# Own buffers and early loads for the opening weights, squares of x on ScalarE, in a hybrid decoder layer

## The chip, the cores and the metric

The kernel runs on one core of a Trainium2 chip. A core has TensorE (PE: matmuls; PEld: its weight loads), VectorE (DVE), ScalarE (ACT), GpSimd (POOL) and SyncE (SP, which here only issues DMAs), each with its own queue that it works through in order. Semaphores tie the queues together. 16 DMA engines move data from the main memory (HBM) into the on-chip memory (SBUF); matmuls write into PSUM banks.

The metric is the device time of one execution in microseconds, the median of several runs. Lower is better.

## What is computed

One decoder layer in float32 on 256 tokens of width 2048. The opening that is changed here is the first step of the mixer: a norm of x and the projection of the normed x.

```python
def rms_norm(x, g):
    xf = x.astype(jnp.float32)
    y = xf * lax.rsqrt(jnp.mean(xf * xf, axis=-1, keepdims=True) + RMS_EPS)
    return (y * g).astype(x.dtype)
...
    proj = h @ w_in
    mlstm_p, rwkv_p, gate_p = split_cols(proj, (MLSTM_TOTAL, RWKV_TOTAL, GATE_TOTAL))
...
for l in range(DEPTH):
    h = rms_norm(x, mix_pre_norm[l])
    y = hybrid_mixer(h, ...)
    x = x + rms_norm(y, mix_post_norm[l])
    h = rms_norm(x, xattn_pre_norm[l])
    m = rms_norm(mem, mem_norm[l])
    x = x + rms_norm(cross_attention(h, m, ...), xattn_post_norm[l])
    h = rms_norm(x, ffn_pre_norm[l])
    x = x + rms_norm(conv_glu_ffn(h, ...), ffn_post_norm[l])
```

`w_in` has 10536 columns. 384 of them, the narrow ones (the ranks of the RWKV decay, its rate and its gate, and the mLSTM gates, padded), are gathered into an own tensor `w_sm`. They are the opening block.

## The kernel before

**Products.** Features lie on the 128 partitions, so x is 16 feature tiles of 128 x 256 tokens. Every float32 product is made of three matmuls with a high and a low half of each operand: high x high, high weights x low x, low weights x high x. The halves of x are `hh` and `hl`, made by `split_gain` (L235): ScalarE writes the high half, `x * gain` rounded, and VectorE subtracts it from `x * gain`. The halves of a weight chunk are `wh` and `wl`, made by `Feed.hi` (L343, a ScalarE cast) and `Feed.lo` (L352, a VectorE subtraction). The norm's division comes after the projection: the squares of x are summed beside the products (`st0`, a `Stat`), and the evacuation multiplies the PSUM banks by the reciprocal root.

**Blocks and chunks.** The program is a list of blocks, one after the other. Each has a list of weight chunks (`srcs`), the x halves, and an evacuation. The opening block (L1278) has 8 chunks of 2 feature tiles x 384 columns (384 KB); the next ones, of `w_in`, 8 chunks of 2 x 512 columns (512 KB). `run` (L369) goes through the chunks and writes out the order of every queue: at chunk i it calls the block's `pre` hook, makes the halves up to chunk i + 1 and then i + 3, asks for the DMA of chunk i + 6, and then issues the matmuls of chunk i.

**Loads.** `Feed.dma` (L324) puts every chunk into one of three shared buffers (tag `raw`). SP issues the loads in program order, and a load waits until the subtraction (L357) of the chunk three before it has read the buffer. x comes in 8 loads of 2 feature tiles (`x_load`, L471). `run` starts with four loads of x and three of weights alternately; the others are issued in the first call of the hook and later.

**The hook.** `pre_sm` (L474) first issues 12 calls of a dummy matmul (`keep_warm`), then for the first three chunks the split of x, the split of the weights, and the next loads, and from then on one split of x per chunk (three chunks ahead). `x_piece` (L459) has, beside the splits, the squares: GpSimd multiplies two feature tiles by themselves (L464, L467) and adds them to the sum (L468).

**Side work.** Evacuations and the chains behind them are generators. `Spread.half` (L103) is called twice per chunk and takes one piece of the first of them, as long as a running account of ScalarE's and VectorE's time allows. `sm_evac` (L508) is the opening block's: it folds the sum (`Stat.finish`), waits three pieces, sums over partitions with TensorE (`st`), waits three more, spreads the root over the partitions (`stb`, `rb`), and then works on the two banks. The tag `big` has two buffers, which the kernel first uses for `KR` and `BK` in the evacuation of a later block (L691).

**The parameters** (`par`, 189 columns; the first 16 are the gain `mixg`) come with one load on ScalarE's queue (L193), the constants `con` and the two halves of `up` with loads that the hooks place between the chunks' (L486, L490, L492).

Of the kernel before, what the change touches and what calls it, by code (L numbers as in the profile page):

```python
# [9 lines left out]
F32 = mybir.dt.float32  # L10
# [5 lines left out]
P = 128  # L16
# [20 lines left out]
NPAR = _o  # L37
# [108 lines left out]
def _layer(ctx, tc, nc, d, dbg):  # L146
    act, dve = Meter(nc.scalar, 200.0, 0.83), Meter(nc.vector, 70.0, 1.04)
# [14 lines left out]
    def big(name, shape=None, dt=F32):  # L162
        return mp.tile(shape or [P, KD, S], dt, tag="big", bufs=2, name=name)
# [19 lines left out]
    def keep_warm(n):  # L183

        q = aux("warm", [P, P])
        for _ in range(n):
            mm(q, ones.broadcast_to((P, P)), ones.broadcast_to((P, P)))
# [2 lines left out]
    x0 = [U("x0"), U("x1")]  # L190
    xq = [x0[c // 4][:, c % 4 * 2:c % 4 * 2 + 2] for c in range(8)]
    par = cp.tile([P, NPAR], F32, name="par")
    act.dma_start(par, d["par"])  # L193
    con = cp.tile([P, NCON], F32, name="con")
    up = C("up", "bg0", [P, 1024])

    def pcol(n, i=0, w=1):
        return par[:, PC[n] + i:PC[n] + i + w]
# [36 lines left out]
    def split_gain(hi, lo, src, g):  # L235
        act.activation(hi, src, AF.Identity, scale=g)
        dve.scalar_tensor_tensor(lo, src, g, hi, op0=ALU.mult, op1=ALU.subtract)
# [80 lines left out]
    class Feed:  # L318
        def __init__(self):
            self.src = [s for b in blocks for s in b["srcs"]]  # L320
            self.kind = [b["kind"] for b in blocks for s in b["srcs"]]
            self.raw, self.st, self.nd, self.ns, self.nl = {}, {}, 0, 0, 0

        def dma(self, upto):  # L324
            while self.nd <= min(upto, len(self.src) - 1):
                s = self.src[self.nd]
                r = wp.tile(list(s.shape), F32, tag="raw", bufs=3, name="raw")
                sp.dma_start(r, s)
                self.raw[self.nd] = r
                self.nd += 1  # L330
# [12 lines left out]
        def hi(self, upto):  # L343
            while self.ns <= min(upto, len(self.src) - 1):
# [4 lines left out]
                self.st[self.ns] = [wh, None]  # L349
                self.ns += 1  # L350

        def lo(self, upto):  # L352
            self.hi(upto)
            while self.nl <= min(upto, len(self.src) - 1):
                r = self.raw.pop(self.nl)
                wl = self.staged("wl", r, self.nl)
                nc.vector.tensor_sub(wl, r, self.st[self.nl][0])  # L357
                self.st[self.nl][1] = wl
                self.nl += 1
# [8 lines left out]

    def run():  # L369
        feed = Feed()  # L370
        for c in range(4):
            x_load(c)
            feed.dma(min(c, 2))
        i = 0
        pend = []
        for b in blocks:
            if len(pend) >= 2:
                side.need(pend[-2])
            if b["before"]:
                b["before"]()  # L380
            nm = b["cols"] // P
            if b["kind"] == "fm":
                banks = [b["pool"]("fm", [P, 2, S]) for _ in range((nm + 1) // 2)]
            else:
                banks = [b["pool"]("tm") for _ in range(2 * (b["cols"] // 512))]
            nk = sum(s.shape[1] for s in b["srcs"])
            k = 0
            nt = len(b["srcs"]) if b["bankwise"] else b["tail"]
            if nt:
                b["srcs"], tail = b["srcs"][:-nt], b["srcs"][-nt:]  # L390
            for ci, s in enumerate(b["srcs"]):
                if b["pre"]:
                    b["pre"](ci, feed)
                feed.lo(i + 1)
                side.half()
                side.more = lambda: feed.hi(i + 2)
                ahead = b["xs"](k)
                feed.lo(i + 3)
                feed.dma(i + 6)
                wh, wl = feed.st.pop(i)  # L400
                for kj in range(s.shape[1]):
                    xh, xl = b["xs"](k) if kj else ahead
                    first, last = k == 0, k == nk - 1
                    if b["kind"] == "fm":
                        for m in range(nm):
                            o = banks[m // 2][:, m % 2]
                            a, c = wh[:, kj, m * P:(m + 1) * P], wl[:, kj, m * P:(m + 1) * P]
                            mm(o, a, xh, start=(first and m % 2 == 0), stop=False)
                            mm(o, a, xl, start=False, stop=False)
                            mm(o, c, xh, start=False, stop=last)  # L410
                            if nm == 8 and m == 3:
                                side.half()
                    else:
                        for g, o in enumerate(banks):
                            tm_products(o, g * P * 512 // b["cols"], g * 512 % b["cols"], (wh[:, kj], wl[:, kj], xh, xl),
                                        first, last)
                            if len(banks) == 4 and g == 1:
                                side.half()
                    k += 1
                    if kj + 1 < s.shape[1]:  # L420
                        side.half()
                i += 1
            if nt:

                feed.lo(i + nt - 1)
                steps = []
                for s in tail:
                    w = feed.st.pop(i)
                    for kj in range(s.shape[1]):
                        steps.append((w[0][:, kj], w[1][:, kj]) + tuple(b["xs"](k)))  # L430
                        k += 1
                    i += 1
                for g, o in enumerate(banks):
                    for si, (wh, wl, xh, xl) in enumerate(steps):
                        if b["kind"] == "tm":
                            tm_products(o, g * P * 512 // b["cols"], g * 512 % b["cols"], (wh, wl, xh, xl), False,
                                        si == len(steps) - 1)
                        for m in range(2 if b["kind"] == "fm" else 0):
                            c = slice((g * 2 + m) * P, (g * 2 + m + 1) * P)
                            mm(o[:, m], wh[:, c], xh, start=(b["bankwise"] and si == 0 and m == 0), stop=False)  # L440
                            mm(o[:, m], wh[:, c], xl, start=False, stop=False)
                            mm(o[:, m], wl[:, c], xh, start=False, stop=si == len(steps) - 1)
                        if si % 2:
                            side.half()
                    if g == 0:
                        feed.lo(i + 1)
                feed.dma(i + 4)
            b["task"] = side.add(b["evac"](banks))
            pend.append(b["task"])
# [6 lines left out]
    xs0 = lambda k: (hh[:, k], hl[:, k])  # L456
    st0 = Stat("st0")

    def x_piece(c):  # L459
        for j in range(2):  # L460
            split_gain(hh[:, c * 2 + j], hl[:, c * 2 + j], xq[c][:, j], pcol("mixg", c * 2 + j))
        if c == 0:
            st0.start()
            pool.tensor_mul(st0.acc, xq[c], xq[c])  # L464
        else:
            q = st0.square()
            pool.tensor_mul(q, xq[c], xq[c])  # L467
            pool.tensor_add(st0.acc, st0.acc, q)  # L468
        st0.n += 1

    def x_load(c):  # L471
        sp.dma_start(xq[c], d["x"][:, c * 2:c * 2 + 2])

    def pre_sm(ci, feed):  # L474
        if ci == 0:
            keep_warm(12)
            for c in range(3):
                x_piece(c)
                feed.lo(c)
                feed.dma(c + 3)  # L480
                x_load(c + 4)
            x_load(7)
        if ci + 3 < 8:
            x_piece(ci + 3)
        if ci == 4:
            sp.dma_start(con, d["con"])  # L486

# [20 lines left out]
    def sm_evac(ps):  # L508
        dve.tensor_scalar(om, pcol("mu", 0, 27), -1.0, 1.0, op0=ALU.mult, op1=ALU.add)
        dve.tensor_scalar(oka, pcol("ka", 0, 8), -1.0, 1.0, op0=ALU.mult, op1=ALU.add)  # L510
        yield from st0.finish(3)
        pr = PR()
        dve.tensor_mul(pr, ps[0], bc(st0.rb, 2))
        wa, gl = C("wa", "m0"), T2("gl")
        gl0, gl1 = gl[:, 0], gl[:, 1]
        shiftmix(wa, pr[:, 0], 24)
        shiftmix(gl0, pr[:, 1], 25)
        yield
        pr = PR()
        dve.tensor_mul(pr[:, 0], ps[1][:, 0], st0.rb)  # L520
        shiftmix(gl1, pr[:, 0], 26, slice(0, 32))
        R = [T2("rows") for _ in range(4)]
        M["rows"] = R
        tasks["gates"] = side.add(gates(), chain=1)
        act.copy(R[0][0:4, 0], pr[32:36, 0])
        act.copy(R[0][0:4, 1], pr[64:68, 0])
        act.activation(wa[0:64], wa[0:64], AF.Tanh)
        tasks["smr"] = side.add(sm_rest(wa, gl0, gl1), back=True)
        yield
# [1194 lines left out]
```

## Time and profile before

| | |
|---|---|
| median of 3 runs | 1940.54 us (1940.47 to 1940.81) |
| the profiled execution | 1939.58 us, of which 1937.6 us are the span from the first to the last instruction |
| TensorE matmul busy | 1900.6 us, 98% of the span |
| VectorE, ScalarE, GpSimd busy | 68%, 52%, 7% |
| moved by DMA | 352.20 MB, a mean of 182 GB/s |
| mean granted TensorE clock | 0.995 |

The profile is of one execution. An engine's busy time is the time in which one of its instructions ran; issuing a DMA does not count. "DMA share" is how busy the 16 DMA engines were. In a row of the timeline stand the start, the duration, the engine (an added q means its queue, as in a DMA issue), the line of the kernel, the operation, the tile that is written and those that are read, the shape, and in brackets the idle time before it with what ended it. Because most instructions go through a few helpers, the tile's name says more than the line.

### The profile page before, as it was taken

The numbers are of one execution on the slowest core, as the hardware profiler recorded it, in microseconds if no ns is written. First come the engines' busy times: TensorE is split into PE (matmuls) and PEld (weight loads), VectorE is DVE, ScalarE is ACT, GpSimd is POOL, SyncE is SP. The second block draws the span as 40 slices with busy tenths as digits, with TensorE's granted clock in tenths as the row PEclk, the third lists the DMA queues.
The fourth block names the chain that finished last, engine by engine and source line by source line (L and its number), as shares of the span: only waits on it lengthen the run. The fifth ranks groups of instructions, "written<-read, shape, count | busy, mean of one in ns | idle before, by whom it ended". The sixth has DMA issues, their size and how long they took to land.

```text
span 1937.6 us, 36532 instructions
## 1 busy us (share of the span) xinstructions
PE 1900.6 (98%) x15084; PEld 1798.7 (93%) x15084; DVE 1326.1 (68%) x1789; ACT 1001.6 (52%) x1434; POOL 137.1 (7%) x127
## 2 busy tenths in 40 slices
PE   7999999999999999899999999999999999999998
PEld 7999987999999999789999999999999998888886
DVE  7879886566566665867767666776667675556555
ACT  4776535544454565555555445544455454455553
POOL 4213100010100000304000000000000000000000
PEclk9999999999999999999999999999999999999999
DMA  6555555344465675435555555556555555655554
GB/s 200 177 163 165 185 164 162 110 142 142 157 183 185 209 261 185 157 133 171 182 186 191 195 196 192 191 190 200 191 194 189 195 195 195 215 192 192 194 195 152
DMA packets 97606, 352.20 MB, mean 182 GB/s; under 512 B 10880, under 2 KB 11136, under 8 KB 97056
## 3 DMA queue, kind: packets, MB, share of 16 engines
q1 hardware_dynamic: 96496, 348.07, 55.0%
q8 instruction: 118, 1.93, 0.4%
q10 hardware_dynamic: 720, 1.15, 0.2%
q0 software_dynamic: 224, 0.66, 0.1%
q14 instruction: 48, 0.39, 0.1%
HBM read 347.73 MB, written 2.10 MB: 181 GB/s over the span
## 4 chain that ended last, share of the span: by engine, by line
PE 87%; DVE 5%; ACT 2%; issue 2%; DMA 2%; POOL 1%; DVEq 0%; SPq 0%; ACTq 0%; POOLq 0%
PE fm L181 59%; PE tm L181 23%; DVE wl L357 2%; ACT wh L348 1%; DMA raw<-in_w_in_dram 1%; DVE fl L66 1%; PE Y L181 1%; DMA raw<-in_w_fu_dram 0%; PE gram L181 0%; PE lv L181 0%; DVE z L66 0%; POOL xr L1225 0%; POOL stx L264 0%; DMA x<-in_x_dram 0%; DVE BK L66 0%
## 5 line engine op out<-in xcount | busy, mean ns | idle before, releaser
L357 DVE TENSOR_TENSOR wl<-raw,wh 128x1024 fp32r<-128x1024 f32 (+1 forms) x648 | 809.6, 1251 | 448.5 <-ACT wh L348 445.4
L348 ACT CAST wh<-raw 128x1024 fp32r<-128x1024 f32 (+1 forms) x648 | 675.7, 1046 | 562.1 <-PE fm L181 373.2
L181 PE MATMUL fm<-fl,wh 128*128 128x256 f32 x2048 | 568.3, 278 | 1.0 <-DVE fl L66 1.0
L181 PE MATMUL fm<-fh,wh 128*128 128x256 f32 x2048 | 568.7, 278 | 0.2 <-ACT fh L66 0.2
L181 PE MATMUL fm<-fh,wl 128*128 128x256 f32 x2048 | 567.7, 277 | 0.0
L181 PEld LDWEIGHTS fm<-fl,wh 128*128 128x128 f32 x2048 | 386.0, 188 | 1.8 <-DVE fl L66 1.7
L181 PEld LDWEIGHTS fm<-fh,wh 128*128 128x128 f32 x2048 | 386.0, 188 | 0.5 <-ACT fh L66 0.5
L181 PEld LDWEIGHTS fm<-fh,wl 128*128 128x128 f32 x2048 | 386.0, 188 | 0.0
L181 PE MATMUL tm<-wh,as 128*128 128x512 f32 x1024 | 315.5, 389 | 0.0
L181 PE MATMUL fm<-hh,wl 128*128 128x256 f32 x1072 | 301.7, 281 | 11.9 <-DVE wl L357 11.9
L181 PE MATMUL fm<-hh,wh 128*128 128x256 f32 x1072 | 305.5, 285 | 1.1 <-ACT wh L348 1.1
L181 PE MATMUL fm<-hl,wh 128*128 128x256 f32 x1072 | 300.7, 280 | 0.0
L181 PEld LDWEIGHTS tm<-wh,as 128*128 128x128 f32 x1024 | 192.1, 188 | 39.8
L181 PEld LDWEIGHTS fm<-hh,wl 128*128 128x128 f32 x1072 | 203.8, 190 | 13.8 <-DVE wl L357 13.8
L181 PEld LDWEIGHTS fm<-hh,wh 128*128 128x128 f32 x1072 | 204.0, 190 | 4.1 <-ACT wh L348 1.5
L181 PEld LDWEIGHTS fm<-hl,wh 128*128 128x128 f32 x1072 | 204.2, 190 | 0.1
L181 PE MATMUL tm<-wl,as 128*128 128x512 f32 x512 | 199.3, 389 | 0.0
L181 PEld LDWEIGHTS tm<-wl,as 128*128 128x128 f32 x512 | 96.1, 188 | 20.0
L66 ACT CAST as<-ac 128x256 fp32r<-128x256 f32 x128 | 45.6, 404 | 112.9 <-PE tm L181 112.9
L66 DVE TENSOR_TENSOR as<-ac,as 128x256 fp32r<-128x256 f32 x128 | 48.6, 422 | 61.7 <-ACT as L66 61.6
L225 POOL TENSOR_TENSOR rco<-var,mhalf 128x1 f32<-128x1 f32 x2 | 1.1, 551 | 1011.6 <-DVE var L66 1011.6
L181 PE MATMUL fm<-mgh,wh 128*128 128x256 f32 x256 | 71.4, 279 | 0.0
(363 smaller groups left out, 2323.6 us busy)
## 6 DMA issues: line engine op xcount, KB each, us to landing
raw<-in_w_fu_dram SPq DMA_DIRECT2D x256, 512.0 KB, 4.2
raw<-in_w_in_dram SPq DMA_DIRECT2D x160, 512.0 KB, 3.7
raw<-in_w_fd_dram SPq DMA_DIRECT2D x128, 512.0 KB, 4.2
raw<-in_w_br_dram SPq DMA_DIRECT2D x32, 512.0 KB, 3.8
raw<-in_w_mo_dram SPq DMA_DIRECT2D x32, 512.0 KB, 4.3
raw<-in_w_xk_dram SPq DMA_DIRECT2D x8, 512.0 KB, 4.5
raw<-in_w_xq_dram SPq DMA_DIRECT2D x8, 512.0 KB, 3.6
raw<-in_w_xv_dram SPq DMA_DIRECT2D x8, 512.0 KB, 4.1
```

What stands on the lines that cost most here:

```text
L66: return f(out, *a, **k)
L181: pe.matmul(out, lhsT, rhs, start=start, stop=stop, skip_group_check=True)
L225: pool.tensor_tensor(out, v, mhalf[:, 0:out.shape[1]], op=ALU.pow)
L348: nc.scalar.copy(wh, r)
L357: nc.vector.tensor_sub(wl, r, self.st[self.nl][0])
```

## The change

It has four parts. The opening block's eight weight chunks get places in two `big` buffers, four chunks in each, and do not use the shared `raw` buffers. `run` issues all eight loads of x and all eight of these weights first, alternately. The opening chunk's halves are made by feature tiles (`Feed.first`): VectorE, not ScalarE, copies the first tile's high half, and the dummy matmuls are 8 calls and not 12. The squares of x leave GpSimd for `Stat.add` (a ScalarE square and a VectorE addition), two loads of x at a time in the hook of chunks 5, 6 and 7, and the last two as two pieces at the head of the evacuation. The load of the parameters becomes two, the 16 gains first.

```diff
-    act.dma_start(par, d["par"])
+    act.dma_start(par[:, 0:16], d["par"][:, 0:16])
+    act.dma_start(par[:, 16:NPAR], d["par"][:, 16:NPAR])
...
+            self.sm = [big(f"wsm{i}", [P, 4, 2, 384]) for i in range(2)]
+
         def dma(self, upto):
             while self.nd <= min(upto, len(self.src) - 1):
                 s = self.src[self.nd]
-                r = wp.tile(list(s.shape), F32, tag="raw", bufs=3, name="raw")
+                if self.nd < 8:
+                    r = self.sm[self.nd // 4][:, self.nd % 4]
+                else:
+                    r = wp.tile(list(s.shape), F32, tag="raw", bufs=3, name="raw")
...
+        def first(self):
+
+            r, wh, wl = self.raw.pop(0), self.staged("wh", self.src[0], 0), self.staged("wl", self.src[0], 0)
+            nc.vector.tensor_copy(wh[:, 0], r[:, 0])
+            for kj in range(2):
+                x_split(0, kj)
+                if kj:
+                    nc.scalar.copy(wh[:, 1], r[:, 1])
+                nc.vector.tensor_sub(wl[:, kj], r[:, kj], wh[:, kj])
+            self.st[0] = [wh, wl]
+            self.ns = self.nl = 1
...
-        for c in range(4):
+        for c in range(8):
             x_load(c)
-            feed.dma(min(c, 2))
+            feed.dma(c)
...
+    def x_split(c, j):
+        split_gain(hh[:, c * 2 + j], hl[:, c * 2 + j], xq[c][:, j], pcol("mixg", c * 2 + j))
+
     def x_piece(c):
         for j in range(2):
-            split_gain(hh[:, c * 2 + j], hl[:, c * 2 + j], xq[c][:, j], pcol("mixg", c * 2 + j))
-        if c == 0:
-            st0.start()
-            pool.tensor_mul(st0.acc, xq[c], xq[c])
-        else:
-            q = st0.square()
-            pool.tensor_mul(q, xq[c], xq[c])
-            pool.tensor_add(st0.acc, st0.acc, q)
-        st0.n += 1
+            x_split(c, j)
...
         if ci == 0:
-            keep_warm(12)
-            for c in range(3):
+            keep_warm(8)
+            feed.first()
+            for c in range(1, 3):
                 x_piece(c)
                 feed.lo(c)
-                feed.dma(c + 3)
-                x_load(c + 4)
-            x_load(7)
         if ci + 3 < 8:
             x_piece(ci + 3)
+        else:
+
+            for c in range((ci - 5) * 2, (ci - 5) * 2 + 2):
+                st0.add(xq[c])
...
     def sm_evac(ps):
...
+        for c in (6, 7):
+            st0.add(xq[c])
+            yield
         yield from st0.finish(3)
```

## The prediction

> **What bounds the kernel now.** The page comes first. TensorE is busy nearly all the span and owns most of the chain that ended last, so time is won only where TensorE stands still or runs slowly.
>
> ```profile
> span 1937.6 us, 36532 instructions
> ...
> PE 1900.6 (98%) x15084; PEld 1798.7 (93%) x15084; DVE 1326.1 (68%) x1789; ACT 1001.6 (52%) x1434; POOL 137.1 (7%) x127
> ...
> PE 87%; DVE 5%; ACT 2%; issue 2%; DMA 2%; POOL 1%; DVEq 0%; SPq 0%; ACTq 0%; POOLq 0%
> ```
>
> 98% is an average over stages, so the second view is the table of windows over the opening. Its columns are the window, busy time and instructions begun of PE, PEld, DVE, ACT and POOL, then the granted clock, the DMA share and GB/s.
>
> ```profile
> 5.00:10.00 5.00, 3.55 (x27) 3.05 (x25) 4.14 (x5) 4.29 (x9) 3.46 (x4) 1.00 0.99 361
> ...
> 6.70:34.95 28.25, 20.36 (x144) 19.26 (x144) 26.51 (x23) 12.63 (x22) 19.81 (x14) 0.88 0.57 184
> ...
> 18.55:21.96 3.41, 1.40 (x13) 1.20 (x12) 3.41 (x3) 1.64 (x3) 3.33 (x3) 1.00 0.58 204
> ...
> 21.96:28.79 6.83, 5.61 (x27) 5.31 (x26) 6.83 (x6) 1.67 (x4) 5.61 (x5) 0.50 0.36 114
> ...
> 30.00:35.00 5.00, 5.00 (x47) 5.00 (x46) 3.43 (x5) 1.05 (x1) 0.00 (x0) 1.00 0.74 237
> ```
>
> The opening block has 8 chunks of 2 feature tiles x 3 column tiles x 3 products = 18 matmuls, 144 in all, and the second row shows those 144 spread over 28.25 us. VectorE is busy in 26.51 of them: it is the engine that paces this stage, not TensorE. The fourth row shows that TensorE also ran at a granted clock of 0.50 for 6.83 us.
>
> Who held TensorE is in the waits (us in total, times, longest), of 6 to 34.95 us and then of 34.95 to 66.5 us:
>
> ```profile
> PE fm L181 <- DVE wl L357: 7.9, 5, 2.2
> ```
>
> ```profile
> PE fm L181 <- DVE wl L357: 1.8, 3, 0.8
> PE stb L181 <- POOL st_c L225: 0.8, 1, 0.8
> PE st L181 <- DVE st L66: 0.8, 1, 0.8
> ```
>
> So nearly all of it is the low half of a weight chunk (wl) coming late from VectorE. The timeline says why:
>
> ```profile
> 16.46 2.69 DVE L66 SCALAR_TENSOR_TENSOR hl<-x,par,hh 128x256 fp32r<-128x256 f32 x2
> 19.07 1.79 DVE L357 TENSOR_TENSOR wl<-raw,wh 128x768 fp32r<-128x768 f32 x1
> ...
> 26.39 1.34 POOL L468 TENSOR_TENSOR st<-st,sq 128x512 f32<-128x512 f32 x1
> ...
> 28.81 0.87 DVE L66 SCALAR_TENSOR_TENSOR hl<-x,par,hh 128x256 fp32r<-128x256 f32 x2
> 29.60 0.94 DVE L357 TENSOR_TENSOR wl<-raw,wh 128x768 fp32r<-128x768 f32 x1
> ```
>
> The same pair of instructions costs VectorE 2.69 + 1.79 = 4.48 us per chunk while GpSimd squares x, and 0.87 + 0.94 = 1.81 us once GpSimd's last addition has ended (26.39 + 1.34 = 27.73). TensorE's own need, from the end of the block at full clock:
>
> ```profile
> 28.82 0.28 PE L181 MATMUL fm<-hh,wl 128*128 128x256 f32 x1
> ...
> 34.95 0.28 PE L181 MATMUL fm<-hh,wl 128*128 128x256 f32 x1
> ```
>
> These are products 89 and 143 (counted from 0); 54 steps in 6.13 us are 0.1135 us each, 2.04 us per chunk. With slow VectorE a chunk costs 4.48, with free VectorE 2.04.
>
> **The change part by part.**
>
> *Squares leave GpSimd.* The 15 GpSimd squares and additions of the stage go. VectorE's cost per chunk falls to 1.81 us, below TensorE's 2.04. The squares become 8 ScalarE squares and 7 VectorE additions, two chunks of x at a time in the pre-steps of chunks 5, 6 and 7 and the last two in the evacuation. Rows of the same forms elsewhere in this kernel:
>
> ```profile
> L66 ACT ACTIVATE sq<-xr 128x512 f32<-128x512 f32 x14 | 8.7, 624 | 2.9 <-POOL stf L264 2.9
> ...
> L66 DVE TENSOR_TENSOR st<-st,sq 128x512 f32<-128x512 f32 x6 | 4.1, 689 | 1.5 <-ACT sq L66 1.5
> ```
>
> That is 8 x 0.62 = 5.0 us of ScalarE and 7 x 0.69 = 4.8 us of VectorE, placed after the splits of x. A table load that Square might need is not excluded; one costs
>
> ```profile
> 1.18 1.28 ACT L66 ACT_TABLE_LOAD   x1 [1.18 <-PEq L1716]
> ```
>
> so 0 to 1.28 us of ScalarE. I take 0: this one set serves all of ScalarE's functions in the old opening, and a load at the squares' place would eat into a margin given below, not into the block itself.
>
> *Weights of the block get buffers, and all loads go out at once.* Before, every load after the third waited for a buffer that a wl freed (SP's queue: start, duration):
>
> ```profile
> 7.67 0.33 SPq L328 DMA_DIRECT2D raw<-in_w_sm_dram  x1
> ...
> 20.88 4.88 SPq L328 DMA_DIRECT2D raw<-in_w_sm_dram  x2
> 28.91 1.99 SPq L328 DMA_DIRECT2D raw<-in_w_in_dram  x2
> ```
>
> Now SP issues x and w alternately, 16 loads, and behind them, with no wait, the first three chunks of the next block (the three shared buffers are still empty). The longest issue among the old first seven:
>
> ```profile
> 3.07 1.39 SPq L328 DMA_DIRECT2D raw<-in_w_sm_dram  x1
> ```
>
> Were every weight issue that long, they would still go out faster than the data arrives. The loads arrive at the queue's rate. A pair is 256 + 384 KB = 655,360 bytes; at the 361 GB/s of the saturated window (share 0.99) 1.82 us, again under 2.04. The start is fixed by rows that the change does not move, as the first seven issues keep their order:
>
> ```profile
> 1.65 5.64 DMA x<-in_x_dram
> ```
>
> ```profile
> 1.18 0.42 SPq L328 DMA_DIRECT2D raw<-in_w_sm_dram  x1
> ...
> 5.82 0.83 ACT L348 CAST wh<-raw 128x768 fp32r<-128x768 f32 x1
> ...
> 9.01 0.91 ACT L66 ACTIVATE hh<-x,par 128x256 fp32r<-128x256 f32 x2
> ```
>
> and, of the DMA view of that first weight load (KB, us to landing),
>
> ```profile
> raw<-in_w_sm_dram SPq DMA_DIRECT2D x1, 384.0 KB, 4.6
> ```
>
> The second chunk of x is there at 7.29, its weights 393,216 / 361e3 = 1.09 us later at 8.38; cast 0.83, subtraction 0.94: wl of chunk 1 at 10.2. ScalarE's 0.91 + 0.83 = 1.74 per chunk also fits under 2.04.
>
> *The first chunk by feature tiles.* Its weights land at 1.18 + 4.6 = 5.78. VectorE's copy now stands ahead of the first hl, and everything on VectorE waits behind it until then. Half-chunk forms (128x384) do not occur before; between the 0.42 us of a 256-wide and the 0.69 of a 512-wide one I take 0.55. Copy, hl (0.44), wl: the third product starts at 7.3 instead of 7.70, the second tile's at 8.3, the chunk is done at 9.1.
>
> ```profile
> 48.31 0.42 DVE L66 COPY st_b<-stb 128x256 f32<-128x256 f32 x1
> ...
> 7.70 0.38 PE L181 MATMUL fm<-hh,wl 128*128 128x256 f32 x1 [0.49 <-DVE wl L357]
> ...
> 12.04 0.39 PE L181 MATMUL fm<-hh,wl 128*128 128x256 f32 x1 [1.94 <-DVE wl L357]
> ```
>
> Chunk 1 cannot go on before 10.2, so this edit, and the split of the parameter load with it, buys nothing at the end; if the order backfires by under 1.1 us it costs nothing either. I take 0.
>
> *The sum.* Product 20 (chunk 1's third) starts at 10.2 instead of 12.04. From there 123 products at 0.1135 are 14.0 us, where the old ones took 34.95 - 12.04 = 22.9. The last product starts at 24.2 instead of 34.95: **10.8 us**.
>
> Does the next block follow? Its loads land at 7.29 + 1.09 + 6 x 1.82 = 19.3 for the last opening chunk, then 512 KB each 1.45 us: 20.7, 22.2, 23.6. Its first cast stands on ScalarE behind chunk 7's cast (20.1) and two squares (21.3):
>
> ```profile
> 32.54 1.05 ACT L348 CAST wh<-raw 128x1024 fp32r<-128x1024 f32 x1 [2.95 <-DMA raw<-in_w_in_dram]
> ...
> 33.62 1.23 DVE L357 TENSOR_TENSOR wl<-raw,wh 128x1024 fp32r<-128x1024 f32 x1 [1.42 <-ACT wh L348]
> ...
> raw<-in_w_in_dram SPq DMA_DIRECT2D x14, 512.0 KB, 4.5
> ```
>
> Cast to 22.4, wl to 23.6, needed at 24.3: the thinnest margin, 0.7 us. The two after it gain on TensorE, which takes 24 products a chunk, 2.7 us. The fourth is issued when the first buffer is free (23.6), lands 4.5 us later and is split at 30.4, needed at 32.5. The loads of con and of the two up-projections keep their places between the same issues.
>
> *What is late next.* The statistics come later by two half-chunk pieces, as two additions stand ahead of the fold. The waits of st, stb and wl after 34.95 (3.4 us together) are tied to that chain and to VectorE's queue; with more lead they may go, or stay two pieces later. I take them as staying, and keep 3.4 us as gain and about 2 as loss. The same shift moves every later side task by up to two half-chunks (2.7 us of TensorE). The largest wait there, in the waits of 160 to 180 us, may go or double:
>
> ```profile
> PE fm L181 <- DVE wl L357: 2.2, 1, 2.2
> ```
>
> So -2.2 to +2.2. The profiled execution took 1939.58 us (span 1937.6), 10.8 less is 1928.8. The median of the runs was 0.96 above it; **1929.7** is the forecast.
>
> **The rivals.**
>
> *The clock.* In the windows above it fell to 0.50 right after a stretch in which TensorE was busy 1.40 of 3.41 us (41%). In the new order the stretch from 4.89 to 8.30 holds about 1.8 us of products (53%), so it is near that edge, and the warm-up is a third shorter. Half clock from 8.30 to 11.72 would cost the 9.7 products it leaves undone, 1.1 us; to 15.13 23.7 of them, 2.7: 1930.8 to 1932.4. Against it: stretches with 53 to 57% kept 1.00 before.
>
> ```profile
> 4.89:8.30 3.41, 1.96 (x15) 1.57 (x14) 2.44 (x4) 2.59 (x6) 1.95 (x2) 1.00 0.99 357
> 8.30:11.72 3.42, 1.80 (x16) 1.59 (x14) 3.42 (x3) 3.42 (x7) 3.26 (x4) 1.00 0.77 283
> ```
>
> The Trainium skill ("TensorE: Matmul & The Clock Gate", Part 1) speaks for this rival: the array starts throttled and is released after a busy window of about 3.4 us on a free-running counter, so a warm-up cut from 12 to 8 calls may miss the release. No run here shows the shorter warm-up.
>
> *A slower queue.* With other loads than the first the windows show 237 GB/s (30 to 35 us). At that rate a pair takes 2.77 us, chunk 7's weights land at 25.6, its third product at 27.3, the block ends at 29.1: 5.9 us gained, 1934.6. Against it: those windows had at most three loads in flight, share 0.74; the saturated one ran at 361.
>
> *Given back downstream.* The two pieces' shift meets the wait of 2.2 us, and adds another like it with a half-clock stretch behind it (3.4 us lost per 6.83): about 5.6 back, 1935.3.
>
> *Slower than before.* If it isn't GpSimd but something else that makes VectorE slow while the opening runs (the landing loads, say), the new order keeps 4.48 us per chunk: chunk 7's third product at 10.2 + 6 x 4.48 = 37.1, the end at 38.8, 3.8 late: 1944.3. It decides from (34.95 - 10.2 - 1.7) / 6 = 3.84 us per chunk. Against it: VectorE is fast at 237 GB/s (30 to 35 us) and slow at 114.
>
> *It doesn't do what it says*, the loads still waiting for buffers: VectorE's relief alone, some 5 us less with chunks at the pace of a load's round trip, or nothing.
>
> **How the numbers follow.** Forecast 0.50; clock 0.20; slower queue 0.08; given back 0.10; slower 0.03; not as said 0.04 (half of it no change); more than forecast, as the later waits go too, 0.05. The range reaches from the forecast less 3.4 and part of the 2.2 (1925.2) to just past the clock and the doubled wait: 1935.0. It leaves out about 2 in 10. A measurement of this kernel can tell 0.2%, 3.9 us: faster 0.92, same 0.05, slower 0.03. (Given back counts as no change for 0.03, not as said for 0.02.)
>
> **What would show it.** Right: hl pairs near 0.87 and wl near 0.94 from the first chunk on, no GpSimd square, the last opening product near 24 us, no wait on wl over 1 us between 10 and 24 us, 8 opening loads issued by about 15 us. Wrong: VectorE still at 4.48 per chunk; a clock of 0.50 before 24 us; ScalarE waiting for opening loads chunk after chunk; new waits of several us after 60 us.

## The result and the profile after

| | before | changed |
|---|---|---|
| median | 1940.51 us (1939.85 to 1940.81, 4 runs) | 1925.79 us (1924.0 to 1927.68, 4 runs) |
| ratio | | 0.9925, 95% interval 0.9912 to 0.9938 |
| profiled execution | 1939.58 us, span 1937.6 | 1927.68 us, span 1925.9 |

The changed kernel is faster by 14.7 us in the medians and by 11.7 in the two profiled spans; its profiled execution is the longest of its four. The forecast was 1929.7, the range 1925.2 to 1935.0.

The page of the changed kernel, span, busy time and shares of the chain that ended last:

```profile
span 1925.9 us, 36521 instructions
...
PE 1900.4 (99%) x15076; PEld 1800.7 (93%) x15076; DVE 1316.9 (68%) x1798; ACT 1007.3 (52%) x1442; POOL 119.8 (6%) x112
...
PE 92%; DVE 3%; DMA 1%; issue 1%; ACT 1%; POOL 1%; DVEq 0%; SPq 0%; ACTq 0%; POOLq 0%
```

TensorE is busy for as long as before (1900.4 against 1900.6 us). The span lost time in which it stood still, which is why the chain's share on it rose. Its windows over the opening (busy time and instructions of PE, PEld, DVE, ACT, POOL, then clock, DMA share, GB/s):

```profile
5.00:10.00 5.00, 3.96 (x17) 3.76 (x18) 4.46 (x11) 4.36 (x9) 0.00 (x0) 1.00 1.03 393
10.00:15.00 5.00, 5.00 (x44) 5.00 (x44) 5.00 (x11) 4.89 (x10) 0.00 (x0) 1.00 1.04 396
15.00:20.00 5.00, 5.00 (x45) 5.00 (x45) 4.94 (x9) 4.26 (x8) 0.00 (x0) 1.00 1.04 405
20.00:25.00 5.00, 5.00 (x47) 5.00 (x46) 3.57 (x4) 4.59 (x7) 0.00 (x0) 1.00 0.39 115
```

GpSimd does nothing there, TensorE is full from 10 us on, and the loads come at 393 to 405 GB/s. VectorE's timeline of the changed kernel:

```profile
5.54 0.36 DVE L361 CAST wh<-wsm 128x384 fp32r<-128x384 f32 x1 [5.54 <-DMA wsm<-in_w_sm_dram]
...
7.54 0.87 DVE L66 SCALAR_TENSOR_TENSOR hl<-x,par,hh 128x256 fp32r<-128x256 f32 x2
8.33 0.95 DVE L375 TENSOR_TENSOR wl<-wsm,wh 128x768 fp32r<-128x768 f32 x1
...
18.30 0.95 DVE L375 TENSOR_TENSOR wl<-wsm,wh 128x768 fp32r<-128x768 f32 x1
...
21.33 1.23 DVE L375 TENSOR_TENSOR wl<-raw,wh 128x1024 fp32r<-128x1024 f32 x1 [1.34 <-ACT wh L354]
```

The pair of hl and wl costs 1.82 us from chunk 1 on, where it was 4.48. The next block's first wl is done at 22.56, two microseconds ahead of the last opening product and so of its own use. TensorE's timeline, products 0, 3, 4, 20 and 143 of the opening:

```profile
6.04 0.55 PE L181 MATMUL fm<-hh,wh 128*128 128x256 f32 x1 [1.32 <-ACT wh L365]
...
7.20 0.42 PE L181 MATMUL fm<-hh,wh 128*128 128x256 f32 x1
7.41 0.41 PE L181 MATMUL fm<-hl,wh 128*128 128x256 f32 x1
...
10.64 0.28 PE L181 MATMUL fm<-hh,wl 128*128 128x256 f32 x1
...
24.72 0.28 PE L181 MATMUL fm<-hh,wl 128*128 128x256 f32 x1
```

Product 20 came at 10.64 (10.2 forecast), the last at 24.72 (24.2 forecast, 34.95 before). From 20 to 143 there are 14.08 us, 0.1145 a step: TensorE's own pace. Products 3 and 4 stand 0.21 apart, where the full clock has 0.1135; 0.21 is also the step of the same products in the stretch of clock 0.50 at 904.7 us, shown below. So TensorE ran at half clock here, until about 10.4 us. The clock column shows 1.00 there all the same: the steps tell more than the column at the very start. SP's queue shows the last two weight loads of the opening and the first of the next block:

```profile
9.04 0.33 SPq L334 DMA_DIRECT2D wsm<-in_w_sm_dram  x1
...
10.68 0.33 SPq L334 DMA_DIRECT2D wsm<-in_w_sm_dram  x1
11.35 1.30 SPq L334 DMA_DIRECT2D raw<-in_w_in_dram  x2
```

**Where the rest went.** The opening's end moved by 34.95 - 24.72 = 10.2 us, the span by 11.7. To find what lies between, one row per kernel is enough, the products of the mixer's output (durations min/median/max, then first and last start), of before and of the changed kernel:

```profile
L181 PE MATMUL fm<-mgh,wh x256: 275/276/365, 667.3 to 756.3; 128*128 128x256 f32 x128
```

```profile
L181 PE MATMUL fm<-mgh,wh x256: 277/283/364, 650.7 to 742.9; 128*128 128x256 f32 x128
```

| stretch | before | changed | difference |
|---|---|---|---|
| start to the last opening product | 34.95 | 24.72 | -10.2 |
| from there to the first product of the mixer's output | 632.4 | 626.0 | -6.4 |
| the mixer's output | 89.0 | 92.2 | +3.2 |
| from its last product to the end of the span | 1181.3 | 1183.0 | +1.7 |

The mixer gained 6.4 us more, its output lost 3.2. TensorE's waits in the mixer (total, times, longest), before from 34.95 to 440 us and changed from 24.72 to 440:

```profile
PE fm L181 <- DVE wl L357: 4.0, 4, 2.2
PE gram L181 <- DVE bg L66: 1.8, 1, 1.8
PE bon L181 <- DVE hsl L66: 0.8, 1, 0.8
PE stb L181 <- POOL st_c L225: 0.8, 1, 0.8
PE st L181 <- DVE st L66: 0.8, 1, 0.8
```

```profile
PE bon L181 <- DVE hsl L66: 2.0, 1, 2.0
PE fm L181 <- DVE wl L375: 1.0, 2, 0.7
PE gram L181 <- ACT bg L66: 0.7, 1, 0.7
```

8.2 us of waits became 3.7 (`gram`, `bon` and `hsl` are tiles of the mixer's chains). From the last opening product to the first of the mixer's output TensorE was idle for 8.3 us before and for 3.7 in the changed kernel, 4.6 of the 6.4; its busy time fell by the other 1.8. Behind the wait on gram, before had a stretch of half clock; its window, columns as above:

```profile
428.10:431.51 3.41, 3.41 (x17) 3.35 (x16) 3.13 (x6) 0.00 (x0) 0.00 (x0) 0.51 0.63 184
```

At half clock for 3.41 us at most 1.7 us are lost. That need not be what the busy time fell by: the changed kernel has a stretch of 3.4 us at 0.50 too, from 208.4 us, behind its wait of 2.0 on bon. Where those 1.8 us came from stays open.

The +1.7 of the last row lies in the feed-forward products (tile `fh`): from the first to the last of them pass 710.4 us before (870.1 to 1580.5) and 712.2 in the changed kernel (856.6 to 1568.8). Before has a stretch of half clock where they begin, the changed kernel one in their midst. The windows of before and of the changed kernel, columns as above:

```profile
868.50:875.30 6.80, 6.38 (x28) 5.79 (x28) 6.80 (x14) 4.01 (x8) 1.72 (x2) 0.50 0.01 2
```

```profile
904.70:908.10 3.40, 3.40 (x18) 3.40 (x17) 1.22 (x1) 1.04 (x1) 0.69 (x1) 0.50 0.67 240
```

The second costs 1.7 us, with TensorE busy all through. All 14 profiled executions of this document divide this way: the eleven with a stretch of half clock in the midst of these products take 712.1 to 712.8 us for them, the three without it 710.4 to 710.9. Those three are before, the run with all squares inside the block and the one with the old loads and the first chunk by tiles. What decides on the stretch was not tried.

### The profile page after: what moved, and what is told of

Same layout as the page of the kernel before. It is cut to its first block, busy times and chain, and to the rows that moved or that the text cites. A ratio compares the mean times of both kernels' runs of the same rounds, so it can differ in the third digit from the quotient of the medians.

```text
span 1925.9 us, 36521 instructions
## 1 busy us (share of the span) xinstructions
PE 1900.4 (99%) x15076; PEld 1800.7 (93%) x15076; DVE 1316.9 (68%) x1798; ACT 1007.3 (52%) x1442; POOL 119.8 (6%) x112
## 4 chain that ended last, share of the span: by engine, by line
PE 92%; DVE 3%; DMA 1%; issue 1%; ACT 1%; POOL 1%; DVEq 0%; SPq 0%; ACTq 0%; POOLq 0%
PE fm L181 64%; PE tm L181 23%; DVE wl L375 1%; DVE fl L66 1%; PE Y L181 1%; ACT wh L354 1%; DMA raw<-in_w_fu_dram 0%; PE gram L181 0%; DMA raw<-in_w_in_dram 0%; PE lv L181 0%; DMA raw<-in_w_xv_dram 0%; POOL xr L1243 0%; DVE z L66 0%; POOL stx L265 0%; PE num L181 0%
## 5 line engine op out<-in xcount | busy, mean ns | idle before, releaser
L375 DVE TENSOR_TENSOR wl<-raw,wh 128x1024 fp32r<-128x1024 f32 x640 | 797.3, 1248 | 447.9 <-ACT wh L354 446.7
L354 ACT CAST wh<-raw 128x1024 fp32r<-128x1024 f32 x640 | 669.2, 1048 | 553.0 <-PE fm L181 382.0
L181 PE MATMUL fm<-mgl,wh 128*128 128x256 f32 x256 | 72.3, 282 | 0.0
```

The source lines that it names most:

```text
L181: pe.matmul(out, lhsT, rhs, start=start, stop=stop, skip_group_check=True)
L354: nc.scalar.copy(wh, r)
```

## The experiments

The changed kernel's four parts were taken apart. The kernel before ran beside each group: 1939.24 us for the first four runs, 1939.2 for the next four, 1938.93 for the two after them and 1941.96 for the last two. Times across groups are therefore compared by their ratios too.

**The changed kernel again, and with 12 dummy matmuls.** The first has no edit; the second:

```diff
-            keep_warm(8)
+            keep_warm(12)
```

> The changed kernel again, unchanged. Its four runs lay 3.7 us apart (1924.0 to 1927.7), those of before under 1 us. Theory (clock phase): the granted clock's windows fall differently against the program in each run, and stretches of half clock (one of 3.4 us costs 1.7) come and go, so the runs again lie 2 to 4 us apart and another profile shows another set of half-clock stretches. Rival: the first four were an accident; the runs lie within 1 us and the profile shows the same stretches. Median 1925 to 1927 in both.

> The changed kernel with 12 warm-up calls in place of 8. Theory: the shorter warm-up (3.3 us of dummy products) does not fill a window of the clock's monitor, so the first products run at half clock until 10.4 us; with 12 calls the full clock is granted by 7 us, the last opening product starts 0.8 to 1.2 us earlier (about 23.3 against 24.4), median 1 us lower. Rival: the clock does not hang on the warm-up; products before 10 us still 0.21 us apart, no difference.

1926.22 us (ratio 0.9929, 0.9917 to 0.9942) and 1926.69 (0.9934, 0.9921 to 0.9946). Products 20 and 143, first the repetition, then 12 calls:

```profile
10.09 0.39 PE L181 MATMUL fm<-hh,wl 128*128 128x256 f32 x1 [0.49 <-DVE wl L375]
...
24.29 0.28 PE L181 MATMUL fm<-hh,wl 128*128 128x256 f32 x1
```

```profile
9.61 0.38 PE L181 MATMUL fm<-hh,wl 128*128 128x256 f32 x1 [0.49 <-DVE wl L375]
...
23.80 0.28 PE L181 MATMUL fm<-hh,wl 128*128 128x256 f32 x1
```

The runs of the repetition lie 2.6 us apart (1924.47 to 1927.09), and it has no half clock at 208 us: such stretches come and go, as expected. In it the clock was full from 4.65 us, and the end came 0.4 us sooner than in the first profile; with 12 calls 0.9 sooner, as expected, but not the time, of which 1 us less was expected. By the steps of the first products, 6 of 8 profiled executions with 8 calls (in all the kernels here) ran at half clock to 10 us or later, and none of 6 with 12 calls did.

**The squares alone**: the kernel before, with its 12 dummy matmuls, three shared buffers and late loads, and only the squares moved.

```diff
 x_piece:
-        if c == 0:
-            st0.start()
-            pool.tensor_mul(st0.acc, xq[c], xq[c])
...
 pre_sm:
+        else:
+            for c in range((ci - 5) * 2, (ci - 5) * 2 + 2):
+                st0.add(xq[c])
 sm_evac:
+        for c in (6, 7):
+            st0.add(xq[c])
+            yield
```

> Before, with only the squares of x moved as in the change (ScalarE squares, VectorE additions, late); loads, buffers, first chunk, warm-up and parameter load as before. Theory (GpSimd's squares slowed VectorE): pairs of hl near 0.87 and wl near 0.94 from the start; a buffer's round trip of issue 0.35, landing 3.1, cast 0.83, subtraction 0.94 is 5.2 us for three buffers, 1.7 a chunk, under TensorE's 2.04; the last opening product starts at 24 to 26 us, so 9 to 11 us gained, 1929 to 1932. Rival (the loads' waits for buffers pace the block): VectorE is fast but waits; the block ends after 31 us, under 4 us gained, 1936.5 or more.

1924.98 us, ratio 0.9926 (0.9913 to 0.994): the whole gain, and 4 us below the 1929 that was the least expected, because waits behind the opening went as well. Its VectorE timeline, ScalarE's, and TensorE's last opening product:

```profile
11.18 0.88 DVE L66 SCALAR_TENSOR_TENSOR hl<-x,par,hh 128x256 fp32r<-128x256 f32 x2
11.97 0.95 DVE L357 TENSOR_TENSOR wl<-raw,wh 128x768 fp32r<-128x768 f32 x1
```

```profile
14.22 0.83 ACT L348 CAST wh<-raw 128x768 fp32r<-128x768 f32 x1 [1.58 <-DMA raw<-in_w_sm_dram]
```

```profile
24.84 0.28 PE L181 MATMUL fm<-hh,wl 128*128 128x256 f32 x1
```

ScalarE still waits for a load (1.58 us), as there are three buffers, but VectorE has so much slack now that the opening ends 0.1 us after the changed kernel's. That one began at half clock, however; the changed kernel with 12 calls, at full clock as this one, ends its opening at 23.80. So the early loads and the two small parts are worth 1.0 us of opening together.

**All but the squares**: the changed kernel with the squares and their sums left on GpSimd, as `x_piece` had them, and the edits of `pre_sm`'s else branch and of `sm_evac` taken out.

> The change with the squares of x left on GpSimd as before; buffers, early loads, first chunk, warm-up and parameter load of the change. Theory: VectorE stays at 4.4 us a chunk until GpSimd is through (about 27 us), the block ends at 32 to 35 us, 0 to 3 us gained, 1937.5 to 1941. Rival (early loads carry it): VectorE is not what counts; the block ends by 27 us, 8 us or more gained, 1932 or less.

1940.1 us, ratio 1.0009 (1.0 to 1.0018): nothing is left of the gain. (It carries some 3 us that come with the tag `big`, shown further below.) Its VectorE timeline, GpSimd's, and TensorE's last opening product:

```profile
5.95 0.48 DVE L66 SCALAR_TENSOR_TENSOR hl<-x,par,hh 128x256 fp32r<-128x256 f32 x1
...
6.81 1.26 DVE L66 SCALAR_TENSOR_TENSOR hl<-x,par,hh 128x256 fp32r<-128x256 f32 x1
...
22.75 2.68 DVE L66 SCALAR_TENSOR_TENSOR hl<-x,par,hh 128x256 fp32r<-128x256 f32 x2
25.36 2.02 DVE L375 TENSOR_TENSOR wl<-wsm,wh 128x768 fp32r<-128x768 f32 x1
27.31 0.87 DVE L66 SCALAR_TENSOR_TENSOR hl<-x,par,hh 128x256 fp32r<-128x256 f32 x2
```

```profile
6.37 1.43 POOL L486 TENSOR_TENSOR sq<-x 128x512 f32<-128x512 f32 x1 [0.84 <-DMA x<-in_x_dram]
...
25.23 1.33 POOL L487 TENSOR_TENSOR st<-st,sq 128x512 f32<-128x512 f32 x1
```

```profile
37.05 0.28 PE L181 MATMUL fm<-hh,wl 128*128 128x256 f32 x1
```

The opening ends later than the 32 to 35 us expected. The same instruction takes 0.48 us in a gap of GpSimd's work (0.84 us idle up to 6.37) and 1.26 beside it; the pair 2.68 + 2.02 until GpSimd ends at 26.56, 0.87 right after. This agrees with the Trainium skill ("SBUF — State Buffer", section "SBUF: two separate sides"), by which a VectorE instruction with two SBUF inputs and a GpSimd instruction that reads SBUF lock each other out of a shared pair of ports for a whole instruction.

**No first chunk by tiles; one load of the parameters.** Each is the changed kernel with one edit undone.

```diff
-            feed.first()
-            for c in range(1, 3):
+            for c in range(3):
```

```diff
-    act.dma_start(par[:, 0:16], d["par"][:, 0:16])
-    act.dma_start(par[:, 16:NPAR], d["par"][:, 16:NPAR])
+    act.dma_start(par, d["par"])
```

> The changed kernel without the method first: chunk 0 is split and staged whole, as chunks 1 and 2 are. Theory (VectorE's pace after chunk 0 sets the end of the opening, the first chunk by tiles is worth nothing there): first product up to 0.8 us later than the 5.9 to 6.0 us of the changed kernel, last opening product still at 24.3 to 25.0 us, time within 1 us of the changed kernel's 1926. Rival (the start of the products is what the end follows): the last opening product moves by the full amount that the first one moves, and the time by as much.

> The changed kernel with the parameters loaded in one transfer. Theory: the first x split waits for x and not for the parameters, so that the first product stays within 0.3 us of 5.9 to 6.0 us, the last opening product at 24.2 to 24.8 us and the time within 1 us of 1926. Rival (the short load lets the first split start sooner): first product 0.5 us or more later, and the end with it.

1926.01 us (ratio 0.9928, 0.9915 to 0.994) and 1924.35 (0.9923, 0.991 to 0.9935). Without the first chunk by tiles the first product starts at 6.43 and the last at 25.10, each 0.4 us late. With one parameter load they start at 6.04 and 24.63, as in the changed kernel. Neither is worth anything that the time can show.

**All squares inside the block**: the run of the squares alone, without the two pieces behind the block, so that the statistics are finished in their old place.

```diff
-        else:
-            for c in range((ci - 5) * 2, (ci - 5) * 2 + 2):
+        if ci >= 4:
+            for c in range((ci - 4) * 2, (ci - 4) * 2 + 2):
                 st0.add(xq[c])
...
-        for c in (6, 7):
-            st0.add(xq[c])
-            yield
```

> The kernel before with the squares of x moved from GpSimd to ScalarE and VectorE as in the run that moved only them, but all eight inside the opening block (chunks 4 to 7 take two each), with no extra pieces behind the block, so that the statistics are finished in the old piece. Theory A (the statistics being finished two half-chunks later moved the mixer's work off the waits at 169 us (2.2) and 427 us (1.8) and the half clock behind the latter): last opening product near 24.8 us as in the run that moved only the squares, but these waits come back and the time is 4 to 6 us above that run's 1925, 1929 to 1931. Theory B (the opening's earlier end changed when those waits meet their loads and pieces): the waits stay away and the time stays within 1 us of 1925.

1929.13 us, ratio 0.9947 (0.9933 to 0.9961), 4.2 above the squares alone. Its waits in the mixer from 25.56 us, the last opening product, and the window behind the second of them:

```profile
PE fm L181 <- DVE wl L357: 3.4, 4, 2.2
PE gram L181 <- DVE bg L66: 1.8, 1, 1.8
```

```profile
417.00:420.42 3.42, 3.42 (x19) 3.20 (x17) 3.05 (x6) 0.00 (x0) 0.00 (x0) 0.50 0.69 172
```

Theory A held: the opening ends 0.7 us later, but the wait of 2.2, the wait of 1.8 and the half clock behind it are those of the kernel before. They are not in the squares alone, where the wait on bon has grown instead, to 1.9 us. So the opening itself is worth 10 us (0.9947 is 10.3 us), and two half-chunks of delay of the side work another 4.

**The tag `big` claimed first**: the squares alone, and in the constructor of `Feed`, where the changed kernel claims its two buffers:

```diff
+            for i in range(2):
+                pool.memset(big(f"claim{i}")[:, 0, 0:2], 0.0)
```

> The kernel before with only the squares moved, and the two buffers of the tag big claimed at the start, as the changed kernel claims them, with two columns of each set to zero by GpSimd and used for nothing. Theory (claiming this tag first moves the other buffers to other addresses, and the mixer's output products run at a step of 0.12 us for that reason, and not for the early loads): the stretch from the first product of the mixer's output to the first of the memory block takes 92 to 93 us, not the 89.9 of the run that moved only the squares, and the time is 2 to 3 us above that run's. Rival (the early loads or the split of the first chunk are the cause): it stays at 90 us, and the time at 1925.

**The opening loads in the tag `U`**, which is claimed first in every kernel here:

```diff
-            self.sm = [big(f"wsm{i}", [P, 4, 2, 384]) for i in range(2)]
+            self.sm = [U(f"wsm{i}", [P, 2, 2, 384]) for i in range(4)]
...
-                    r = self.sm[self.nd // 4][:, self.nd % 4]
+                    r = self.sm[self.nd // 2][:, self.nd % 2]
```

> The changed kernel with the eight opening loads in four buffers of the tag U, two pairs of rows in each, in place of two buffers of the tag big: U is the first tag that is claimed in every one of these kernels, and the tag big is claimed as late as in the kernel before. Theory (the claim of big at the start moved the other buffers, and this slows the mixer's output products, not the early loads): the stretch from the first product of the mixer's output to the first of the memory block is 89.5 to 90 us, the opening ends at 24.3 to 24.8 us, the first product of the second mixer half comes at 219 to 222 us as in the changed kernel, and the time is 1922.5 to 1924. Rival (the early loads themselves move the feed's buffers against the products): the stretch stays at 92 to 93 us and the time at 1925 to 1926.5.

1929.43 us (ratio 0.9946, 0.9933 to 0.9958) with the claim, 1923.04 (1921.9 to 1923.58; 0.9915, 0.9901 to 0.9929) with `U`. The products of the mixer's output: squares alone, then the claim, then `U`:

```profile
L181 PE MATMUL fm<-mgh,wh x256: 276/276/364, 651.6 to 741.1; 128*128 128x256 f32 x128
```

```profile
L181 PE MATMUL fm<-mgh,wh x256: 277/283/364, 653.9 to 746.1; 128*128 128x256 f32 x128
```

```profile
L181 PE MATMUL fm<-mgh,wh x256: 276/276/364, 648.3 to 737.4; 128*128 128x256 f32 x128
```

89.5, 92.2 and 89.1 us for the same 768 products. The slow stage comes with the claim alone, without early loads, and goes with early loads in another tag. In all 14 profiles the median is 283 ns where `big` is claimed first (seven) and 276 or 277 where it is not. What the claim changes for these products is where `mgh` and `mgl`, which live in `big`, lie in SBUF. The next products whose moving operand lies in `big`, those of `qh` and `ql` near 780 us, go the same way in the same profiles, 283 for 276 or 277; those of `fh`, which doesn't lie there, have 276 in all. The claim moves other tiles too; that it is the operand's own place is the nearest reading, not a proof. The claim cost more than the 2 to 3 us expected (4.5): its opening also ended later, at 26.11 for 24.84, and ScalarE waits up to 2.56 us for a weight load there, for 1.58 in the squares alone. Why that load came later was not tried.

**First chunk and parameters with the old loads**: the squares alone, with `Feed.first` and the two parameter loads added.

> The kernel before with the squares moved as in the run that moved only them, and the first chunk by feature tiles and the parameters in two transfers, but the old order and buffers of the loads. Theory: the mixer's output stretch stays at 90 us and the first two parts bring at most 0.5 us, so that the time is 1924 to 1925.5. Rival (the first chunk needs the early loads to be worth something, and takes VectorE's time from chunk 1): up to 1 us above 1925.

1926.81 us (1923.73 to 1928.85; 0.9933, 0.992 to 0.9946), above the expected 1924 to 1925.5 and wide. It speaks against a gain from these two parts and doesn't tell nothing from a loss of 1 us.

**The early loads and the squares only**: as with `U`, without `Feed.first` and with one parameter load; beside it the run with `U` again.

> The run with the opening loads in buffers of the tag U, without the method first and with the parameters in one transfer: of the change, the early loads and the squares are left. Theory (first chunk by tiles and two parameter transfers are worth nothing at the end): first product 0.3 to 0.8 us later than with them, last opening product within 0.7 us of 23.7, mixer's output stretch 89.5 to 90 us, time within 1 us of that run's 1923. Rival: each of the two brings its part of the 0.5 to 1 us to the end, and the time is 1924 to 1925.

> The run with the opening loads in buffers of the tag U once more, to see whether its 1923 stands beside the changed kernel's 1926: theory (the place of the tag big costs the changed kernel some 3 us) 1922 to 1924, and the mixer's output stretch at 89.5 to 90 us; rival (the 3 us were the spread of single runs): 1924 to 1927.

1921.78 us (1921.09 to 1923.85; 0.9903, 0.9887 to 0.992) and 1923.02 (1920.66 to 1925.16; 0.9906, 0.9891 to 0.9921). The leaner kernel's first product started at 6.35 and its last opening product at 25.25, where some 23.7 was expected. The 23.74 of the first run with `U` was at full clock; its repetition, at half clock like the leaner kernel, has 5.91 and 24.49. So the two parts are worth 0.4 us at the first product and 0.8 at the last, and still the leaner kernel is not the slower one. It is the fastest version measured; its runs lie below all four of the changed kernel, though the intervals of the ratios meet (0.992 and 0.9912).

## Why the prediction was right, and where its steps failed

The direction and the main term were right, by the mechanism that was named: 10.2 us of opening for 10.8. The time came 3.9 us below the forecast, inside the range, because of terms that the sum had at zero: 6.4 us won in the mixer, 3.2 lost in its output. That these partly cancel, and leave the time in the range, is luck.

1. **VectorE paces the opening because of GpSimd.** Right, and shown from both sides: with the squares gone and all else as before the pair falls to 1.83 us and the opening ends at 24.84; with the squares kept and all else changed it stays at 4.70 and the opening ends at 37.05. This was also the point of the rival on the other side (VectorE slow for another reason), which falls.
2. **Early loads are needed for product 20 at 10.2.** The forecast of the end (24.2) was met within 0.5 us, but not for that reason: with the old loads product 20 stood at 9.88. The early loads are at most 1 us of the 10 (24.84 without them, 23.80 with them and the small parts, both at full clock). The estimate of 361 GB/s was low as well (393 to 405), and the rival of a slower queue had no footing.
3. **First chunk and parameters worth nothing.** Right: 0.4 to 0.8 us of opening at most, nothing in the time.
4. **What is late next.** The next block's first wl, with a margin of 0.7 us, held with 2. The waits behind the opening were mis-sized: the 3.4 us of st, stb and wl were kept as staying, and 1.0 is left. The wait of 2.2 was given -2.2 to +2.2 without a choice, and the one on gram with the half clock behind it was not in the sum. The mixer gained 6.4 us against 0 in the forecast. Two causes show, by which kernels have which wait. The waits of 2.2 on wl and of 1.8 on gram stand in the three profiles whose statistics are finished in the old piece (before, the squares on GpSimd, all squares inside the block) and in none of the eleven with the two added pieces; in those the wait on bon is 1.8 to 2.0 us, where it was 0.2 to 0.8. The prediction had counted this shift mainly as a risk: the rival of a giving back downstream had the mechanism with the wrong sign, and the case of later waits going too had a chance of 0.05. The waits on st and stb are not the shift's: in the five profiles with the old loads they sum to 1.2 to 1.9 us, the squares alone among them, and in the nine with the early loads to 0.2 at most, also with the squares on GpSimd. TensorE's idle time accounts for 4.6 of the 6.4; the other 1.8 are open.
5. **The place of `big`.** Not seen at all: +3.2 us in a stage 600 us later, which hid half of point 4. Without it the forecast would have missed by 7.
6. **The clock.** The rival's event came: after 8 dummy calls the clock was at half to 10.4 us. The Trainium skill ("TensorE: Matmul & The Clock Gate", Part 1) has the full clock granted after a busy window of about 3.4 us, and the window free-running. The trace agrees: 8 calls, 3.8 us of dummy products, left half clock in 6 profiles and not in 2. The rival's price did not come: 0.4 to 0.9 us of opening instead of 1.1 to 2.7, since full clock would have had TensorE wait for VectorE there (0.49 us at product 20 in the repetition). The 9.7 and 23.7 products behind the prediction's price are given without their working; the second window would add 15 by the step of 0.1135, where they add 14.

In one account against before: squares off GpSimd -10, side work two pieces later -4, early loads about -2 (`U` against the squares alone, 1923.04 and 1924.98; in the traces the 1 us of opening and the waits on st and stb, in the time at the edge of what it tells), the place of `big` +3; together -13. The repetition measured -13.0 (1939.24 to 1926.22), the first comparison -14.7.

## What to carry to other kernels

When an engine paces a stage, compare its instructions' durations inside and outside the stage before counting its work: here the work was right and the durations were 2.5 times too long, because of a helper beside it that looks idle on the page (7% of the span). Take a change of several parts apart before keeping it; one of four did nearly all, two did nothing, and one gave back 3 us through a buffer that was claimed early. A shift of side work by a piece or two is worth an experiment of its own, since it can open or close waits of 2 us hundreds of microseconds later.

## What was unexpected of the hardware

- The same 768 products with the same operands had a median of 276 or 277 ns each, or of 283, with the order in which the buffers were claimed, in 14 of 14 profiles; 89.0 to 89.5 us or 92.2 in all (90.4 in one, where TensorE also waited 0.8 us for weights). The place of the moving operand in SBUF changes with it. Which property of the place counts was not tried.
- With loads queued back to back the DMA windows showed 393 to 405 GB/s and shares of 1.03 and 1.04, above the 361 GB/s and 0.99 of the saturated window before.
- A half-clock stretch of 3.4 us can follow a stall of less than 2 us hundreds of microseconds into the kernel: at 417.0 us, behind the wait of 1.8 in the run with all squares inside the block, with TensorE full (3.42 of 3.42 us) while it lasted.
